# Differential attention: scores as two float32r products over stacked halves, blocks in order of heads

## The chip, the core and the metric

The kernel runs on one core of a Trainium2 chip. The metric is the device time of one execution in microseconds (us), the median of the runs; lower is better. A run's time is about 2 us more than the span that the profiler sees between the first and the last instruction.

## What is computed

A block of four mixers with a mixture of experts and two feed-forward parts, T = 512 tokens of width D = 1024, all in float32. The change touches the first mixer alone, differential attention with 8 heads; every head has two components of 64 dimensions for q and k, and a value of 128:

```python
q, k, v = jnp.split(x @ w_in, [2*H*dh, 4*H*dh], axis=-1)          # H = 8, dh = 64
q = rmsnorm(q.reshape(B, T, H, 2, dh), q_gain) * (dh ** -0.5)
k = rmsnorm(k.reshape(B, T, H, 2, dh), k_gain)
v = v.reshape(B, T, H, 2 * dh)
for s in range(0, T, QBLOCK):                                     # QBLOCK = 128
    e = s + QBLOCK
    sc = jnp.einsum('bqhcd,bkhcd->bhcqk', q[:, s:e], k[:, :e])
    dist = (jnp.arange(s, e)[:, None] - jnp.arange(e)[None, :])
    sc = jnp.where(dist >= 0, sc - slopes[:, None, None, None] * dist, -jnp.inf)
    p = jax.nn.softmax(sc, axis=-1)
    pd = p[:, :, 0] - lam * p[:, :, 1]
    outs.append(jnp.einsum('bhqk,bkhe->bqhe', pd, v[:, :e]))
o = rmsnorm(jnp.concatenate(outs, axis=1), subln) * (1.0 - lambda_init)
return o.reshape(B, T, H * 2 * dh) @ w_out
```

## The kernel before, in words

Differential attention is `stage_a` (line 397), the first of the program's stages; the experts follow, then the other mixers and feed-forward parts. TensorE's large products are split: weights and activations are each a high part (rounded to float32r) and a low remainder, and `mm3` (L131) issues three float32r products of 128 rows by 512 columns (in the profile L135 to L137 for products with weights stationary in one form, L139 to L141 in the other). The high part of a weight tile is an ACT copy (`wh`, L110), the low part a DVE subtraction (`wl`, L111). Weights come over the SP queue, 1 MB at a time, into three buffers `wr`.

`stage_a` works on two groups of four heads. `project(G)` (L437) makes q, k and v of a group: q and k are normalized per head component (`headnorm`, L443), transposed on TensorE (L464) and copied by one ACT instruction per block of 128 tokens (L465) into one tile `qt` or `kt` of four heads, each head with component 0 in rows 0 to 63 and component 1 in rows 64 to 127. `attend(G)` (L480) works in units of one block of 128 queries i and one head hh, blocks outermost:

```python
us = [(i, hh) for i in range(NT) for hh in range(4)]              # L552, before
```

A unit's `score` (L483) issues for each component c one float32 product over that component's 64 rows with n = 128(i+1) columns (L490). DVE adds the distance term and takes the minimum (`p<-s`, L491), scales it (L493); ACT takes the exponential (L494); DVE forms the reciprocal (L497, L498), scales (L499) and combines the two components (L500). `turn` (L502) transposes the result (L508) and copies it (L510) one unit later, `value` (L512) multiplies by v (L517) one more later. After the fourth head of a block, `onorm` (L523) normalizes 512 columns that hold one block of queries for four heads (L525 to L533), transposes them (L544) and makes their high and low parts `oh`, `ol` (L546, L547), which the output product `out(G)` needs in full, all four blocks of them, for each of its columns.

The lists of units are interleaved by `weave` (L177): `attend(0)` with all but eight units of `project(1)`; the first four units of `attend(1)` with these eight; the other twelve with `out(0)`, of which a part is kept for after the last unit. Then follow `out(1)` and the router. The order of each engine's instructions is then set by a scheduler in the framework, on which buffers and waits have their effect; so the change also moves instructions that it does not name. From the middle of `out(1)` to the end of the program the order of every engine is the same in both kernels (on PE the last 7316 rows).

`q_stack` (L662), `k_stack` (L672) and `halves` (L650) stand in the program already, for other mixers: `halves` makes the high part of a transposed tile by an ACT copy `nh` (L654) and the low part by a DVE subtraction `nl` (L655), with one buffer each; 64-row pieces of them are copied over the SP queue (128 KB each) into tiles of 128 rows: `qs` holds a component's high part above its low part, `kh` its high part twice, `kl` its low part twice (L667, L668, L682). Their scores are in `soft_heads` (L700): two float32r products of 128 rows, `kh` by `qs` and `kl` by `qs`, into one accumulator.

Of the kernel before, what the change touches and what calls it, by code (L numbers as in the profile page):

```python
# [4 lines left out]
F32 = mybir.dt.float32  # L5
# [3 lines left out]
AF = mybir.ActivationFunctionType  # L9
# [5 lines left out]
T, D, P = 512, 1024, 128  # L15
NT, NK = T // P, D // P
# [65 lines left out]
class K:  # L82
# [314 lines left out]
    def stage_a(self):  # L397
        nc, tc, a = self.nc, self.tc, self.a
        w_in, w_out = a["da_w_in"], a["da_w_out"]
        self.nmm, self.ns, self.ntp, self.npv = 4, 2, 1, 1  # L400
        with tc.tile_pool(name="pa", bufs=1) as pa:
            xv, wv = a["xT"].rearrange("(k p) t -> p k t", p=P), w_in.rearrange("(k p) n -> p k n", p=P)
# [8 lines left out]

            lv = pa.tile([P, 2, 64], F32, name="lv", tag="wk", bufs=7)
            ls = pa.tile([P, 2], F32, name="ls")
# [23 lines left out]
            def project(G, first=None):  # L437
                q = pa.tile([P, 4, T], F32, name="qt", tag="qt", bufs=2)
                k = pa.tile([P, 4, T], F32, name="kt", tag="kt", bufs=2)
                v = pa.tile([P, NT, 512], F32, name="v", tag="v", bufs=2)  # L440
                qkv[G] = (q, k, v)

                def headnorm(dst, gain, slopes=False):  # L443
                    def done(i, ps):
                        rt = self.rt[:, i:i + 1]
                        s = pa.tile([P, 512], F32, name="qs", tag="wk", bufs=7)
# [13 lines left out]

                        def turn():
                            tp = self.ptt()
                            for hh in range(4):
                                nc.tensor.transpose(tp[:, hh * P:(hh + 1) * P], s[:, hh * P:(hh + 1) * P], self.ident)  # L464
                            nc.scalar.activation(dst[:, :, i * P:(i + 1) * P], tp.rearrange("p (a b) -> p a b", a=4),  # L465
                                                 AF.Copy, scale=gain)
                        self.after(8, scale)
                        self.after(12, turn)
                    return done

                def vdone(i, ps):
                    nc.scalar.activation(v[:, i], ps, AF.Copy, scale=self.rt[:, i:i + 1])

                return (self.tm_cols(w_in, G * 512, 512, x, headnorm(q, gs[:, 0:1], True), first)
                        + self.tm_cols(w_in, 1024 + G * 512, 512, x, headnorm(k, self.vec("kg")))
                        + self.tm_cols(w_in, 2048 + G * 512, 512, x, vdone))

            def attend(G):
                q, k, v = qkv[G]
# [32 lines left out]
                def value(i, hh):  # L512
                    if hh == 0:
                        pvs[i] = self.pvt()
                    p = pt.pop((i, hh))
                    for j in range(i + 1):
                        nc.tensor.matmul(pvs[i][:, hh * P:(hh + 1) * P], lhsT=p[:, j * P:(j + 1) * P],  # L517
                                         rhs=v[:, j, hh * P:(hh + 1) * P], start=j == 0, stop=j == i,
                                         skip_group_check=True)
                    if hh == 3:  # L520
                        onorm(i, pvs.pop(i))

                def onorm(i, pv):  # L523
                    s = pa.tile([P, 512], F32, name="os", tag="wk", bufs=7)
                    nc.scalar.copy(s, pv)  # L525
# [11 lines left out]
                    def turn_o():  # L537
                        if G not in o:
                            o[G] = (self.x8("oh"), self.x8("ol"))
                        oh, ol = o[G]  # L540
                        qs = slice(i * P, i * P + P)
                        tp = self.ptt()
                        for hh in range(4):
                            nc.tensor.transpose(tp[:, hh * P:(hh + 1) * P], s[:, hh * P:(hh + 1) * P], self.ident)  # L544
                        tv = tp.rearrange("p (a b) -> p a b", a=4)
                        nc.scalar.activation(oh[:, :, qs], tv, AF.Copy, scale=gs[:, 1:2])  # L546
                        nc.vector.scalar_tensor_tensor(ol[:, :, qs], tv, gs[:, 1:2], oh[:, :, qs].bitcast(F32),  # L547
                                                       op0=OP.mult, op1=OP.subtract)
# [578 lines left out]
    def moe_begin(self, pool):  # L1127
# [12 lines left out]
        o = _CST["four"][0]  # L1140
        f = pool.tile([P, 388], F32, name="cr", tag="wk", bufs=7)
        nc.scalar.dma_start(f, a["cst"][:, o:o + 388])
# [7 lines left out]
    def zero_rows(self, pool):  # L1150

        z = pool.tile([P, T], F32, name="zr", tag="wk", bufs=7)
        self.nc.gpsimd.memset(z, 0.0)
# [4 lines left out]
    def route_step(self, pool):  # L1158
# [4 lines left out]
        def done(m, ps):  # L1163
# [5 lines left out]
            self.sumsq(m)  # L1169
            hg = pool.tile([P, T], F32, name="hg", tag="wk", bufs=7)  # L1170
            nc.scalar.activation(hg, self.h[:, m], AF.Copy, scale=g[:, m:m + 1])

            def turn():
# [9 lines left out]
                for i in range(NT):  # L1183
                    nc.tensor.transpose(tp[:, i * P:(i + 1) * P], hg[:, i * P:(i + 1) * P], self.ident)
                xk = pool.tile([P, T], F32, name="xk", tag="wk", bufs=7)
                nc.scalar.copy(xk, tp)
# [543 lines left out]
```

## Time and profile before

| what | value |
|---|---|
| median of 3 runs | 1909.3 us (1907.06 to 1910.37) |
| the profiled execution | 1910.65 us |
| its span, first to last instruction | 1908.9 us |
| mean granted TensorE clock | 0.988 |
| PE busy over the span | 1835.4 us, 96% |
| DVE, ACT, POOL busy | 69%, 51%, 12% |
| first score product of this attention | at 85.3 us |
| first of the second group of heads | at 181.5 us |
| last score's DVE step begins | at 231.95 us |
| last transposes of the normalized result | at 246.8 us |

PE is TensorE's matmul stream, PEld its weight loads, DVE VectorE, ACT ScalarE, POOL GpSimd, SP the engine whose queue issues most transfers. A busy time is the union of instructions' records; the matmul's recorded end lies after the point at which the next one can begin, so a price for a stretch of matmuls is the distance between starts. A float32 product leaves two records, a float32r product one. A wait has the form "who waits <- for whom".

### The profile page before, as it was taken

Reading aid. Unit: us, or ns where it says so; the run is one execution under the profiler, and the core shown is the slowest. Engines: PE = TensorE matmul, PEld = TensorE weight load, DVE = VectorE, ACT = ScalarE, POOL = GpSimd, SP = SyncE. Lnnn points to the kernel's source line nnn. Section 1 sums busy time; section 2 is a strip of 40 time slices with the busy share of each in tenths; the row PEclk is TensorE's granted clock in tenths of the full one; section 3 lists DMA queues with packets and bytes.
Section 4 is the critical chain, followed back from the end, with each engine's and each line's share of the span. In section 5 each row is a group of like instructions: output and inputs, shape, how many; then the busy total and the mean of one; then the engine's idle time right before and its main releaser. Section 6 shows DMA issues by size and latency. Waiting matters only on the chain.

```text
span 1908.9 us, 24634 instructions
## 1 busy us (share of the span) xinstructions
PE 1835.4 (96%) x8604; PEld 1448.6 (76%) x8605; DVE 1318.4 (69%) x2815; ACT 978.0 (51%) x1663; POOL 226.3 (12%) x277
## 2 busy tenths in 40 slices
PE   8999997999998999998999999999999999999997
PEld 6767685778887876675688888888777788888885
DVE  6586848999998689756677447744576667537753
ACT  5565656888885325346454224433376544324442
POOL 2000012222322302310200000012200100000001
PEclk9999998999999999999999999999999999999998
DMA  5511157999994454454232343234545233243331
GB/s 190 181 45 67 67 172 268 355 369 370 368 366 147 135 148 115 111 147 106 83 96 75 91 114 107 68 95 141 137 112 133 67 90 103 77 119 89 88 85 60
DMA packets 260098, 274.74 MB, mean 144 GB/s; under 512 B 14438, under 2 KB 175622, under 8 KB 259968
## 3 DMA queue, kind: packets, MB, share of 16 engines
q1 hardware_dynamic: 250688, 257.56, 44.1%
q0 software_dynamic: 5072, 10.00, 1.5%
q10 hardware_dynamic: 4208, 5.56, 0.8%
q8 instruction: 69, 1.13, 0.2%
q14 instruction: 61, 0.50, 0.1%
HBM read 238.19 MB, written 15.73 MB: 133 GB/s over the span
## 4 chain that ended last, share of the span: by engine, by line
PE 51%; DVE 2%; ACT 2%; DMA 1%; POOL 1%; SPq 1%; issue 1%; DVEq 0%; POOLq 0%; ACTq 0%
PE mm L137 14%; PE mm L135 14%; PE mm L136 14%; PE pv L727 2%; PE t L715 1%; PE s L700 1%; PE pv L1101 1%; PE mm L140 1%; PE mm L139 1%; PE mm L141 1%; DMA rsw<-qd 0%; SPq L391 0%; POOL rsw L392 0%; PE s L1067 0%; PE t L1086 0%
## 5 line engine op out<-in xcount | busy, mean ns | idle before, releaser
L110 ACT CAST wh<-wr 128x1024 fp32r<-128x1024 f32 (+5 forms) x335 | 306.6, 916 | 442.6 <-PE mm L136 318.8
L111 DVE TENSOR_TENSOR wl<-wr,wh 128x1024 fp32r<-128x1024 f32 (+4 forms) x332 | 356.8, 1078 | 196.4 <-ACT wh L110 193.7
L135 PE MATMUL mm<-xh,wh 128*128 128x512 f32 x952 | 372.9, 392 | 2.1 <-DVE h L384 1.8
L137 PE MATMUL mm<-xh,wl 128*128 128x512 f32 x952 | 372.9, 392 | 0.2 <-DVE wl L111 0.2
L136 PE MATMUL mm<-xl,wh 128*128 128x512 f32 x952 | 371.8, 391 | 0.0
L135 PEld LDWEIGHTS mm<-xh,wh 128*128 128x128 f32 x952 | 179.2, 188 | 40.0 <-issue 3.5
L137 PEld LDWEIGHTS mm<-xh,wl 128*128 128x128 f32 x952 | 179.1, 188 | 38.1 <-issue 1.1
L136 PEld LDWEIGHTS mm<-xl,wh 128*128 128x128 f32 x952 | 179.1, 188 | 36.1 <-issue 0.2
L111 DVE TENSOR_TENSOR wl<-wx,wh 128x1024 fp32r<-128x1024 f32 x123 | 151.3, 1247 | 11.7 <-ACT wh L110 5.6
L110 ACT CAST wh<-wx 128x1024 fp32r<-128x1024 f32 x134 | 139.5, 1050 | 27.6 <-PE mm L141 23.4
L139 PE MATMUL mm<-wh,xh 128*128 128x512 f32 (+2 forms) x352 | 132.0, 380 | 9.7 <-ACT wh L110 5.6
L135 PE MATMUL mm<-hh,wh 128*128 128x512 f32 x352 | 139.0, 395 | 0.0
L136 PE MATMUL mm<-hl,wh 128*128 128x512 f32 x352 | 138.9, 395 | 0.0
L137 PE MATMUL mm<-hh,wl 128*128 128x512 f32 x352 | 138.9, 395 | 0.0
L140 PE MATMUL mm<-wl,xh 128*128 128x512 f32 (+2 forms) x352 | 131.1, 373 | 4.3 <-DVE wl L111 4.2
L141 PE MATMUL mm<-wh,xl 128*128 128x512 f32 (+2 forms) x352 | 129.7, 369 | 0.0
L624 DVE TENSOR_TENSOR z<-mm,rb 128x512 f32<-128x512 f32 x88 | 60.4, 688 | 81.3 <-PE mm L137 81.3
L139 PE MATMUL mm<-wh,xeh 128*128 128x512 f32 x256 | 103.9, 406 | 0.8 <-ACT xeh L1361 0.8
L277 POOL TENSOR_TENSOR acc<-acc,sq 128x512 f32<-128x512 f32 x42 | 58.3, 1388 | 377.2 <-ACT sq L273 376.8
L141 PE MATMUL mm<-wh,xel 128*128 128x512 f32 x256 | 101.8, 398 | 0.0
L140 PE MATMUL mm<-wl,xeh 128*128 128x512 f32 x256 | 101.1, 395 | 0.0
L384 DVE TENSOR_TENSOR h<-mm,h 128x512 f32<-128x512 f32 x88 | 60.5, 690 | 50.4 <-PE mm L137 49.3
(406 smaller groups left out, 3352.3 us busy)
## 6 DMA issues: line engine op xcount, KB each, us to landing
wr<-in_ffn_w_up SPq DMA_DIRECT2D x88, 512.0 KB, 4.9
wx<-in_moe_w_gate SPq DMA_DIRECT2D x23, 1024.0 KB, 8.9
wx<-in_moe_w_up SPq DMA_DIRECT2D x22, 1024.0 KB, 9.7
wx<-in_moe_w_down SPq DMA_DIRECT2D x22, 1024.0 KB, 11.0
wr<-in_ffn_w_down SPq DMA_DIRECT2D x32, 704.0 KB, 4.6
wr<-in_da_w_in SPq DMA_DIRECT2D x11, 1024.0 KB, 5.1
wr<-in_even_w_in SPq DMA_DIRECT2D x11, 1024.0 KB, 5.5
wr<-in_moe_w_up SPq DMA_DIRECT2D x10, 1024.0 KB, 8.0
```

The costliest lines, as they stand in the source:

```text
L110: nc.scalar.copy(h, raw)
L111: (nc.gpsimd if eng else nc.vector).tensor_tensor(l, raw, h.bitcast(F32), op=OP.subtract)
L135: mm(out, lhsT=wh, rhs=xh, start=first, stop=False, skip_group_check=True)
L136: mm(out, lhsT=wh, rhs=xl, start=False, stop=False, skip_group_check=True)
L137: mm(out, lhsT=wl, rhs=xh, start=False, stop=last, skip_group_check=True)
L139: mm(out, lhsT=xh, rhs=wh, start=first, stop=False, skip_group_check=True)
L140: mm(out, lhsT=xh, rhs=wl, start=False, stop=False, skip_group_check=True)
L141: mm(out, lhsT=xl, rhs=wh, start=False, stop=last, skip_group_check=True)
L277: nc.gpsimd.tensor_tensor(self.acc, self.acc, sq, op=OP.add)
L384: self.nc.vector.tensor_tensor(self.h[:, m], ps, self.h[:, m], op=OP.add)
L624: nc.vector.tensor_tensor(z[:, 2:], ps, self.rb, op=OP.mult)
L727: nc.tensor.matmul(pv[64 * e:64 * e + 64, j * P:], lhsT=heads[u]["v"](j), rhs=pt[:, 4 * j:3 * j + 4], start=j == 0, stop=j == NT - 1, skip ...
```

## The change

The scores of differential attention take the form that `soft_heads` has. For every head, q and k are split into high and low halves and copied into stacks; a component's score block is two float32r products of 128 rows. The blocks go in order of heads, each head through its four query blocks; the normalized result is made per head. The tiles `qt` and `kt` hold two heads, three buffers each, so that the copy out of the transposes becomes two instructions. To make room, `p2` has two buffers for three, the work tiles `wk` six for seven, and the scratch for dynamic DMAs 2048 bytes for 8192. A head's stacks are asked for while the head ahead is at its blocks 1 (q) and 2 (k); those of each group's first head after its last k block.

```diff
+        self.nst, self.nsl = 4, 4
             def project(G, first=None):
-                q = pa.tile([P, 4, T], F32, name="qt", tag="qt", bufs=2)
-                k = pa.tile([P, 4, T], F32, name="kt", tag="kt", bufs=2)
+                q, k = [], []
...
-                            nc.scalar.activation(dst[:, :, i * P:(i + 1) * P], tp.rearrange("p (a b) -> p a b", a=4),
-                                                 AF.Copy, scale=gain)
+                            if i == 0:
+                                dst.extend(pa.tile([P, 2, T], F32, name=name, tag=name, bufs=3) for _ in range(2))
+                            for t, c in zip(dst, (0, 2 * P)):
+                                nc.scalar.activation(t[:, :, i * P:(i + 1) * P], tp[:, c:c + 2 * P].rearrange("p (a b) -> p a b", a=2),
+                                                     AF.Copy, scale=gain)
+                            if dst is k and i == NT - 1:
+                                self.after(2, lambda: prep(4 * G, 0))
+                                self.after(6, lambda: prep(4 * G, 1))
...
+            def prep(u, part):
+                t = qkv[u // 4][part][u % 4 // 2][:, u % 2]
+                if part == 0:
+                    stacks[u] = self.q_stack(pa, t)[0]
+                else:
+                    stacks[u] = [(q, *k) for q, k in zip(stacks[u], self.k_stack(pa, t))]
...
-                    p2 = p2s[i, hh] = pa.tile([P, 2, T], F32, name="p2", tag="p2", bufs=3)
+                    if hh < 3 and i in (1, 2):
+                        prep(4 * G + hh + 1, i - 1)
+                    p2 = p2s[i, hh] = pa.tile([P, 2, T], F32, name="p2", tag="p2", bufs=2)
                     for c in range(2):
-                        b = slice(64 * c, 64 * c + 64)
+                        q, *k = stacks[4 * G + hh][c]
                         s = self.pst()
-                        nc.tensor.matmul(s[:, :n], lhsT=q[b, hh, qs], rhs=k[b, hh, :n], start=True, stop=True)
+                        for m, t in enumerate(k):
+                            nc.tensor.matmul(s[:, :n], lhsT=q[:, qs], rhs=t[:, :n], start=m == 0, stop=m == 1)
...
-                    if hh == 3:
-                        onorm(i, pvs.pop(i))
+                    if i == NT - 1:
+                        onorm(hh, pvs.pop(hh))
...
-                us = [(i, hh) for i in range(NT) for hh in range(4)]
+                us = [(i, hh) for hh in range(4) for i in range(NT)]
...
-    nc = bacc.Bacc("TRN2", target_bir_lowering=False, num_devices=1, dynamic_dma_scratch_size=8192)
+    nc = bacc.Bacc("TRN2", target_bir_lowering=False, num_devices=1, dynamic_dma_scratch_size=2048)
```

How the order moves, at three places. In these rows the name left of the arrow is what is written, the names right of it what is read, with the tile's number; the line is that of the kernel concerned (in the changed kernel the score product is L510, the transposes of p2 L528, the value product L537, the transposes of the result L563, the stack copies L685, L686 and L700).

TensorE at the first scores, before: the two components of a unit (`s_841`, `s_846`) stand next to each other, between projection products.

```order
L139 MATMUL mm_678<-wh_768,xh1_108 128x512
L140 MATMUL mm_678<-wl_769,xh1_108 128x512
L141 MATMUL mm_678<-wh_768,xl1_110 128x512
L490 MATMUL s_841<-kt_122,qt_121 128x128
L490 MATMUL s_846<-kt_122,qt_121 128x128
L139 MATMUL mm_866<-wh_862,xh0_107 128x512
```

And in the change, at the same place (288 projection products stand ahead of the first score in both):

```order
L139 MATMUL mm_682<-wh_788,xh1_108 128x512
L140 MATMUL mm_682<-wl_789,xh1_108 128x512
L141 MATMUL mm_682<-wh_788,xl1_110 128x512
L510 MATMUL s_875<-kh_810,qs_776 128x128
L510 MATMUL s_875<-kl_813,qs_776 128x128
L139 MATMUL mm_902<-wh_898,xh0_107 128x512
L510 MATMUL s_881<-kh_816,qs_779 128x128
L140 MATMUL mm_902<-wl_899,xh0_107 128x512
L141 MATMUL mm_902<-wh_898,xl0_109 128x512
L139 MATMUL mm_902<-wh_898,xh0_107 128x512
```

Each component is now a couple of products on stacks that SP's copies must have filled, and projection products stand between them. The second group's first score, 534 projection and output products from the program's start before, has 559 ahead of it now.

TensorE at the end of the second group's attention, before, from one of the last units' transposes on (`t_2455`; its `mm` rows are output products of `out(0)`):

```order
L508 MATMUL t_2455<-ident_70,p2_2411 128x128 x4
L135 MATMUL mm_2507<-oh_1118,wh_2508 128x512
L136 MATMUL mm_2507<-ol_1119,wh_2508 128x512
L137 MATMUL mm_2507<-oh_1118,wl_2509 128x512
L517 MATMUL pv_2495<-v_838,pt_2433 128x128 x4
L517 MATMUL pv_2495<-v_838,pt_2460 128x128 x4
L508 MATMUL t_2488<-ident_70,p2_2438 128x128 x4
L135 MATMUL mm_2559<-oh_1118,wh_2560 128x512
L136 MATMUL mm_2559<-ol_1119,wh_2560 128x512
L137 MATMUL mm_2559<-oh_1118,wl_2561 128x512
L135 MATMUL mm_2559<-oh_1118,wh_2560 128x512
L517 MATMUL pv_2495<-v_838,pt_2493 128x128 x4
```

In the change, from the last score product on:

```order
L510 MATMUL s_2742<-kl_2547,qs_2488 128x512
L537 MATMUL pv_2662<-v_872,pt_2660 128x128
L137 MATMUL mm_2958<-oh_2444,wl_2960 128x512
L528 MATMUL t_2726<-ident_70,p2_2682 128x128 x2
L537 MATMUL pv_2818<-v_872,pt_2703 128x128
L537 MATMUL pv_2818<-v_872,pt_2729 128x128 x2
L528 MATMUL t_2753<-ident_70,p2_2707 128x128 x3
L537 MATMUL pv_2818<-v_872,pt_2757 128x128 x3
L563 MATMUL t_2786<-ident_70,os_2763 128x128 x4
...
L537 MATMUL pv_2818<-v_872,pt_2816 128x128 x4
L563 MATMUL t_2870<-ident_70,os_2829 128x128 x4
```

Between the last score and the last transposes of the result (`t_2870`) seven output products are left; before there were 47.

SP around the second group's first head, in the change (before, SP issues no copies between these loads):

```order
L128 DMA wr_1634<-in_da_w_in 128x4x512
L685 DMA qs_2016<-nh_2012 64x512
L686 DMA qs_2016<-nl_2013 64x512
L685 DMA qs_2019<-nh_2012 64x512
L686 DMA qs_2019<-nl_2013 64x512
L128 DMA wr_2327<-in_da_w_out 128x4x512
L128 DMA wr_2329<-in_da_w_out 128x4x512
L128 DMA wr_2931<-in_da_w_out 128x4x512
L700 DMA kh_2061<-nh_2057 64x512 x2
L700 DMA kl_2064<-nl_2058 64x512 x2
```

The copies of a head's k stack stand behind weight loads that were issued ahead of them on the same queue.

## Rows read from the trace of the kernel before

**Rows 1.** The page: span, busy times, and the clock by slices.
```profile
span 1908.9 us, 24634 instructions
PE 1835.4 (96%) x8604; PEld 1448.6 (76%) x8605; DVE 1318.4 (69%) x2815; ACT 978.0 (51%) x1663; POOL 226.3 (12%) x277
PEclk9999998999999999999999999999999999999998
```

**Rows 2.** Busy time by stretch: the attention's two halves.
```profile
core 0: us, PE busy (x) PEld busy (x) DVE busy (x) ACT busy (x) POOL busy (x), PEclk, DMA share, GB/s
85.00:181.00 96.00, 93.60 (x475) 66.41 (x474) 73.91 (x337) 57.98 (x127) 0.00 (x0) 1.00 0.17 55
181.00:254.00 73.00, 72.47 (x362) 49.95 (x361) 60.35 (x250) 43.32 (x111) 0.00 (x0) 1.00 0.25 83
```

**Rows 3.** The same view, the score products' line alone.
```profile
sum 169.00, PE 32.14 PEld 12.00; mean PE 16.07 PEld 6.00
```

**Rows 4.** Timeline of PE, two neighbouring components, a lone one, the last one.
```profile
130.47 1.13 PE L490 MATMUL s<-kt,qt 64*128 64x512 f32 x4
131.53 0.71 PE L517 MATMUL pv<-v,pt 128*128 128x128 f32 x4
...
226.41 1.12 PE L490 MATMUL s<-kt,qt 64*128 64x512 f32 x2
227.47 0.66 PE L544 MATMUL t<-ident,os 128*128 128x128 f32 x4
228.05 0.69 PE L490 MATMUL s<-kt,qt 64*128 64x512 f32 x1
```

**Rows 5.** Timeline of PE in a later mixer with stacked scores.
```profile
749.57 0.39 PE L700 MATMUL s<-kh,qs 128*128 128x512 f32 x1
749.80 0.39 PE L700 MATMUL s<-kl,qs 128*128 128x512 f32 x1
750.03 0.40 PE L137 MATMUL mm<-xh,wl 128*128 128x512 f32 x1
```

**Rows 6.** Busy time of that line over eight such heads.
```profile
725.00:832.00 107.00, 16.00 (x64) 10.14 (x64) 1.00 0.47 122
```

**Rows 7.** The halves in that mixer: tile nh, durations in ns and waits.
```profile
L654 ACT CAST nh<-qa x4: 603/606/622, 843.6 to 887.3; 128x512 fp32r<-128x512 f32 x4
L655 DVE TENSOR_TENSOR nl<-ka,nh x4: 685/688/689, 849.7 to 892.7; 128x512 fp32r<-128x512 f32 x4
DMA to landing us min/median/max: 2.2/2.4/5.2
```

**Rows 8.** The score tile there: what ended idle time before it (us, times).
```profile
  DMA kl<-nl: 2.4, 2
  DMA kh<-nh: 2.4, 2
```

**Rows 9.** DMA issues: KB each, median us to landing.
```profile
wr<-in_da_w_in SPq DMA_DIRECT2D x11, 1024.0 KB, 5.1
qs<-nh SPq DMA_DIRECT2D x32, 128.0 KB, 2.2
qs<-nl SPq DMA_DIRECT2D x32, 128.0 KB, 2.6
```

**Rows 10.** Timeline of PE behind the last score: output products, last transposes.
```profile
243.14 0.39 PE L137 MATMUL mm<-oh,wl 128*128 128x512 f32 x1
243.36 0.39 PE L135 MATMUL mm<-oh,wh 128*128 128x512 f32 x1
...
246.31 0.39 PE L136 MATMUL mm<-ol,wh 128*128 128x512 f32 x1
246.82 0.63 PE L544 MATMUL t<-ident,os 128*128 128x128 f32 x4
```

**Rows 11.** Timeline of DVE: the last score's step and its result's normalization.
```profile
231.95 0.68 DVE L491 CUSTOM_DVE_ANT_0 p<-s,c_dist 128x512 f32<-128x512 f32 x1
232.56 0.09 DVE L491 DVE_READ_ACCUMULATOR2_ANT st<- 128x1 f32 x1
...
235.68 0.74 DVE L500 SCALAR_TENSOR_TENSOR p<-p,rc 128x512 f32<-128x512 f32 x1
...
240.46 0.69 DVE L529 TENSOR_REDUCE oss<-sq 128x4 f32<-128x512 f32 x1 [1.38 <-ACT sq L527]
...
245.98 0.69 DVE L533 TENSOR_TENSOR os<-os,rsq 128x512 f32<-128x512 f32 x1
```

**Rows 12.** Waits between 84 and 242 us (us, times, longest).
```profile
ACT p L494 <- DVE st L493: 21.7, 27, 4.4
DVE p L491 <- PE s L490: 13.6, 12, 5.4
```

More of the change, by code (lines that the diff above doesn't have):

```diff
@@ L410, in stage_a @@
             nc.sync.dma_start(dist, a["cst"][:, _CST["dist"][0]:_CST["dist"][0] + T])
-            lv = pa.tile([P, 2, 64], F32, name="lv", tag="wk", bufs=7)
+            lv = pa.tile([P, 2, 64], F32, name="lv", tag="wk", bufs=6)
             ls = pa.tile([P, 2], F32, name="ls")
@@ L472, in vdone @@
                     nc.scalar.activation(v[:, i], ps, AF.Copy, scale=self.rt[:, i:i + 1])
-                return (self.tm_cols(w_in, G * 512, 512, x, headnorm(q, gs[:, 0:1], True), first)
-                        + self.tm_cols(w_in, 1024 + G * 512, 512, x, headnorm(k, self.vec("kg")))
+                return (self.tm_cols(w_in, G * 512, 512, x, headnorm(q, "qt", gs[:, 0:1], True), first)
+                        + self.tm_cols(w_in, 1024 + G * 512, 512, x, headnorm(k, "kt", self.vec("kg")))
                         + self.tm_cols(w_in, 2048 + G * 512, 512, x, vdone))
+            stacks = {}
+            def prep(u, part):
[4 more added lines that the diff above has]
+                    stacks[u] = [(q, *k) for q, k in zip(stacks[u], self.k_stack(pa, t))]
             def attend(G):
-                q, k, v = qkv[G]
+                v = qkv[G][2]
                 pvs, pt, p2s = {}, {}, {}
@@ L512, in value, with onorm @@
                 def value(i, hh):
-                    if hh == 0:
-                        pvs[i] = self.pvt()
+                    if i == 0:
+                        pvs[hh] = self.pvt()
                     p = pt.pop((i, hh))
                     for j in range(i + 1):
-                        nc.tensor.matmul(pvs[i][:, hh * P:(hh + 1) * P], lhsT=p[:, j * P:(j + 1) * P],
+                        nc.tensor.matmul(pvs[hh][:, i * P:(i + 1) * P], lhsT=p[:, j * P:(j + 1) * P],
                                          rhs=v[:, j, hh * P:(hh + 1) * P], start=j == 0, stop=j == i,
                                          skip_group_check=True)
-                    if hh == 3:
-                        onorm(i, pvs.pop(i))
-                def onorm(i, pv):
-                    s = pa.tile([P, 512], F32, name="os", tag="wk", bufs=7)
+                    if i == NT - 1:
+                        onorm(hh, pvs.pop(hh))
+                def onorm(hh, pv):
+                    s = pa.tile([P, 512], F32, name="os", tag="wk", bufs=6)
                     nc.scalar.copy(s, pv)
@@ L540, in turn_o @@
                         oh, ol = o[G]
-                        qs = slice(i * P, i * P + P)
                         tp = self.ptt()
[L543 to L547, printed above, removed]
+                        for i in range(4):
+                            nc.tensor.transpose(tp[:, i * P:(i + 1) * P], s[:, i * P:(i + 1) * P], self.ident)
+                        nc.scalar.activation(oh[:, hh], tp, AF.Copy, scale=gs[:, 1:2])
+                        nc.vector.scalar_tensor_tensor(ol[:, hh], tp, gs[:, 1:2], oh[:, hh].bitcast(F32),
                                                        op0=OP.mult, op1=OP.subtract)
@@ L1140, in moe_begin @@
         o = _CST["four"][0]
-        f = pool.tile([P, 388], F32, name="cr", tag="wk", bufs=7)
+        f = pool.tile([P, 388], F32, name="cr", tag="wk", bufs=6)
         nc.scalar.dma_start(f, a["cst"][:, o:o + 388])
@@ L1150, in zero_rows @@
     def zero_rows(self, pool):
-        z = pool.tile([P, T], F32, name="zr", tag="wk", bufs=7)
+        z = pool.tile([P, T], F32, name="zr", tag="wk", bufs=6)
         self.nc.gpsimd.memset(z, 0.0)
@@ L1169, in done @@
             self.sumsq(m)
-            hg = pool.tile([P, T], F32, name="hg", tag="wk", bufs=7)
+            hg = pool.tile([P, T], F32, name="hg", tag="wk", bufs=6)
             nc.scalar.activation(hg, self.h[:, m], AF.Copy, scale=g[:, m:m + 1])
@@ L1184, in turn @@
                     nc.tensor.transpose(tp[:, i * P:(i + 1) * P], hg[:, i * P:(i + 1) * P], self.ident)
-                xk = pool.tile([P, T], F32, name="xk", tag="wk", bufs=7)
+                xk = pool.tile([P, T], F32, name="xk", tag="wk", bufs=6)
                 nc.scalar.copy(xk, tp)
```

4 lines of the change are left out of this document (2 added, 2 removed).

## The prediction

> **What bounds the kernel now.** First the page: PE is busy for 1835.4 of 1908.9 us and its clock stands at its upper level in nearly every slice, while no other engine passes 76% [rows 1]. Time is therefore gained by giving PE less to do, or lost by making it wait. Then the stretches: the change acts between the first score at 85 us and the point, near 254 us, where the attention's last result has gone through PE. There PE is busy for 93.60 of 96.0 us in the first half (four heads) and for 72.47 of 73.0 in the second; DVE stands at 73.91 (77%) and 60.35 (83%) [rows 2]. So PE sets the pace, DVE is next, and in the second half it is near. The clock is 1.00 in both, so no price here mixes levels. Behind this point the order of every engine is the same in both kernels, up to the prefetch of two weight tiles; what is won or lost by 254 us should reach the end as it is, and the sum is made for these 169.0 us alone.
>
> **Scores.** Their line is busy for 32.14 us in the two halves [rows 3]. That is not yet what they cost. In the timeline a unit's two components of 512 columns, four records, start at 130.47 and the next instruction at 131.53, so 1.06 us for both; a lone component, two records, costs 1.06 too (226.41 to 227.47) [rows 4]. Two products over 64 rows each, one in the lower and one in the upper half, thus run side by side when they are neighbours. The record, at 1.13, is longer than the distance by 6%; by the same share the 32.14 are about 30.1 us of PE's time.
>
> The new form is in the trace already, in another mixer: `kh` starts at 749.57, `kl` at 749.80, and the next product at 750.03, so a couple of 512 columns costs 0.46 us and its last record runs 0.16 over into what follows [rows 5]. Eight heads with one component each make 32 couples of all four sizes and are busy for 16.00 us [rows 6]; less 32 times 0.16 for the overrun that is 10.9, and with two components per head 21.8. If every size went by columns at the rate of 512 (0.46 times 10/4 a component, sixteen of them) it would be 18.4. I take 21.1, nearer to the sum over whole heads: the scores lose **9.0 us** (bounds 8.3 and 11.7), half in each half.
>
> [...]
>
> **Making the stacks.** Sixteen ACT casts of 0.61 us and sixteen DVE subtractions of 0.69 [rows 7], 9.8 and 11.0 us in all; DVE's next instruction starts about 0.61 after one of that length (231.95 to 232.56 [rows 11]). Ten subtractions fall into the first half, six into the second. In the first half DVE then has 73.91 + 10 x 0.61 = 80.0 us in some 98: covered. ACT goes from 101.3 of 169 us to some 113 with the halves and eight more copies out of the transposes; covered. The 96 copies of 128 KB over SP land in 2.2 to 2.6 us [rows 7, 9]; with a DMA share of 0.17 and 0.25 [rows 2] the bytes have room. Three costs remain on the path.
>
> *First stacks.* Head 0's copies follow its last k block at once; PE waits for cast, subtraction and landing, about 0.61 + 0.61 + 2.4 and the issue of the later of eight copies, less the projection products that the scheduler put between. In the other mixer the scores waited twice for `kh` and twice for `kl`, 2.4 us in all for each [rows 8]. I take **+1.5** (0 to 4).
>
> *The seam.* `nh` and `nl` have one buffer. At the second group's start three casts (k of head 4, q of head 5, k of head 5) follow each other on ACT with only a few exponentials and copies between; a cast must wait until the copies out of the last one have landed, up to 5.2 us [rows 7], and the exponentials behind it on ACT wait too. Projection and output products stand ready on PE. I take **+1.0** (0 to 4).
>
> *Head order.* Before, the last score's DVE step starts at 231.95, its combined result is done some 4.5 us later, its normalization runs from the reduction at 240.46 to the scaling at 245.98 [rows 11], and the last transposes start at 246.82; below this chain of 14.9 us PE worked through output products every 0.2275 us, with a gap of only some 0.3 us ahead of the transposes [rows 10]. In the new order 7 of the 47 output products behind the last score are left there. The same chain takes perhaps 11.5 us with DVE emptier, at most 14.9 as in the row; PE's work in it is 7 products at 0.2275, 11 value products and 13 transposes at about 0.11 each, 4.3 us. So PE idles for 7.2 to 10.6 us; some of it falls into gaps that it had. I take **+7.0** (5 to 10.6).
>
> **What costs nothing.** The split copy of `qt` and `kt` sits on ACT, which had 43.32 of 73.0 us to do in the fuller half. Six `wk` and two `p2` buffers: a third of `p2` let a score's DVE step run ahead of the transposes; with two, a score waits for the transposes of the one before last. DVE's waits for PE were 13.6 us in all, and ACT's for DVE 21.7 [rows 12]; I put nothing on it apart from what the slower rival holds. The smaller scratch concerns the experts' gathers and scatters on POOL, busy 12% [rows 1]; nothing is counted, and what speaks against it would show at 290 to 580 us, not here.
>
> **The sum.** First half: 96.0, plus 25 products that now stand ahead of the second group's first score (559 against 534, 5.7 us), less 4.5, plus 1.5: 98.7. Second half: 73.0 - 5.7 - 4.5 + 7.0 = 69.8; the seam 1.0. Together 169.5 against 169.0, so **+0.5 us**. DVE in the second half has 60.35 + 6 x 0.61 = 64.0 us in 69.8, 92%: it fits, but barely, and this is the weakest step. The profiled execution is 1910.65 us (1908.9 of span and 1.75 around it); it stands 1.35 above the median of 1909.3, to which I add the difference: 1909.8. Over the bounds, scores at their best with the least of each cost give 1909.3 - 11.7 + 5 = 1902.6; at the worst of each 1909.3 - 8.3 + 4 + 4 + 10.6 = 1919.6.
>
> **Rivals.**
>
> *DVE takes over (slower).* In the second half PE's work is now 62.8 us without the tail, DVE's 64.0. DVE never reached more than 83% of a half; its order is fixed, each unit goes from PE to DVE to ACT and back, and only two `p2` buffers decouple it. The point from which this decides is 64.0/69.8, 92%: if DVE can keep only 83% as in the row, the half takes 64.0/0.83 = 77.1 in place of 69.8, and the time is 1909.8 + 7.3 = 1917. For it: the last score's DVE step at 231.95 [rows 11] came some 3 us after its product at 228.05 [rows 4], so DVE was already behind there. Against it: the 83% were set by PE, not by DVE. Chance 0.22.
>
> *The scores give more, or the tail less (faster).* [...] Chance 0.30, of it 0.08 by the rule.
>
> *Stacks behind weights (slower).* [...] Chance 0.10. [...]
>
> *No effect of the edit itself* is excluded by the order: couples on stacks stand where the old products stood.
>
> **How the numbers follow.** The forecast, 1905 to 1914, has 0.38; faster 0.30, DVE 0.22, late stacks 0.10. A measurement of this kernel tells about 0.2%, 3.8 us, from no change: faster means under 1905.5, slower over 1913.1. Of the forecast's 0.38 some 0.02 falls on each side beyond; the faster cases reach up to 1905.5 and hold 0.29 beyond it; the slower ones hold 0.30. That gives 0.31 faster, 0.36 same, 0.33 slower. The range leaves out the extremes of both sides: 1901 to 1918.
>
> **What would show it.** In the changed profile: the score line busy for about 30 us in the two halves by its records, though 21 by distances between starts (a couple of 512 columns at 0.46); the second group's first score near 184 us; PE idle for 6 to 9 us between the last score and the last transposes of the result; these waits named for ACT or DVE, not DMA. Waits of the score products for `kh`, `kl` or `qs` of more than 4 us in all would show late stacks; DVE at over 90% and PE waiting for its steps in the second half, the DVE rival. The forecast is wrong if the result leaves 1901 to 1918, and its reasons are wrong if a difference arises after 290 us, where the order is the same.

## The result, and the profile after

The changed kernel takes 1922.73 us in the median (1921.63 to 1923.2, 4 runs) against 1909.61 before: slower by 13.1 us, ratio 1.007 with a 95% interval of 1.0053 to 1.0088. That is above the range of 1901 to 1918; the forecast was 0.5 us more.

The page and the stretches of the changed kernel, to be held against [rows 1 to 3]; the last line is the score line alone (columns as there):

```profile
span 1921.4 us, 24892 instructions
PE 1832.6 (95%) x8604; PEld 1463.1 (76%) x8605; DVE 1328.7 (69%) x2831; ACT 986.9 (51%) x1695; POOL 224.2 (12%) x277
...
85.00:181.00 96.00, 93.52 (x492) 76.24 (x493) 79.84 (x349) 62.51 (x143) 0.00 (x0) 0.98 0.45 126
181.00:254.00 73.00, 63.15 (x328) 49.73 (x327) 59.60 (x237) 42.42 (x110) 0.00 (x0) 0.93 0.59 166
...
sum 169.00, PE 31.84 PEld 22.53; mean PE 15.92 PEld 11.27
```

PE is busy for 2.8 us less over the span, part of that at a lower clock, and the span is 12.5 us longer. In the first half PE is as busy as before, with a clock of 0.98 for 1.00. In the second, PE's 72.47 busy us of 73.0 have become 63.15, and the granted clock, 1.00 before, is 0.93.

The new scores at a granted clock of 1.00 (223 to 225 us), from the timeline of PE (start, duration, instruction, idle before):

```profile
223.85 0.40 PE L510 MATMUL s<-kh,qs 128*128 128x512 f32 x1
224.08 0.40 PE L510 MATMUL s<-kl,qs 128*128 128x512 f32 x1
224.32 0.39 PE L537 MATMUL pv<-v,pt 128*128 128x128 f32 x2
```

A couple of 512 columns costs 0.47 us (0.46 in the other mixer [rows 5]). PE waits for the first head's stacks twice, in component 0's `kl` and in component 1's `kh`, 2.53 us together:

```profile
83.16 0.22 PE L510 MATMUL s<-kh,qs 128*128 128x128 f32 x1
85.02 0.33 PE L510 MATMUL s<-kl,qs 128*128 128x128 f32 x1 [1.64 <-DMA kl<-nl]
85.18 0.44 PE L139 MATMUL mm<-wh,xh 128*128 128x512 f32 x1
86.52 0.30 PE L510 MATMUL s<-kh,qs 128*128 128x128 f32 x1 [0.89 <-DMA kh<-nh]
```

Behind these waits the granted clock falls for a while, to 0.70 and 0.50 in the stretches from 86 to 88 and from 88 to 90 us:

```profile
86.00:88.00 2.00, 1.48 (x5) 1.22 (x6) 0.20 (x1) 1.46 (x4) 0.00 (x0) 0.70 0.30 68
88.00:90.00 2.00, 2.00 (x8) 1.71 (x7) 0.96 (x4) 0.49 (x1) 0.00 (x0) 0.50 0.60 137
```

Most of the loss is in the second group of heads. The end of it on PE, from the last score product on:

```profile
241.50 0.40 PE L510 MATMUL s<-kl,qs 128*128 128x512 f32 x1
...
245.11 0.52 PE L528 MATMUL t<-ident,p 128*128 128x128 f32 x3 [1.30 <-DVE st L513]
246.29 0.94 PE L537 MATMUL pv<-v,pt 128*128 128x128 f32 x6 [0.66 <-ACT pt L530]
249.85 1.09 PE L563 MATMUL t<-ident,os 128*128 128x128 f32 x4 [2.62 <-DVE os L553]
251.71 1.22 PE L135 MATMUL mm<-oh,wh 128*128 128x512 f32 x2 [0.78 <-ACT oh L564]
252.73 1.06 PE L528 MATMUL t<-ident,p 128*128 128x128 f32 x4
...
255.29 1.91 PE L537 MATMUL pv<-v,pt 128*128 128x128 f32 x8
262.45 1.08 PE L563 MATMUL t<-ident,os 128*128 128x128 f32 x4 [5.25 <-DVE os L553]
```

And on DVE, to be held against [rows 11]:

```profile
243.75 0.68 DVE L511 CUSTOM_DVE_ANT_0 p<-s,c_dist 128x512 f32<-128x512 f32 x1
...
246.78 0.75 DVE L520 SCALAR_TENSOR_TENSOR p<-p,rc 128x512 f32<-128x512 f32 x1
...
249.01 0.69 DVE L553 TENSOR_TENSOR os<-os,rsq 128x512 f32<-128x512 f32 x1
...
258.52 0.69 DVE L549 TENSOR_REDUCE oss<-sq 128x4 f32<-128x512 f32 x1 [6.08 <-ACT sq L547]
```

The last unit's combined probabilities are ready at 247.5, yet PE transposes them (L528) at 252.73. In PE's order the transposes of the third head's normalized result (L563, 249.85) stand ahead of them, and wait 2.62 us for DVE's scaling at 249.01; then the second output product's first steps wait for that head's high part. Only then comes the last unit, with its value products, copy, normalization and a wait of 5.25 us. From the last score's step on DVE to the last transposes it is 18.7 us, against 14.9 before. The waits between 181 and 266 us say the same (us, times, longest):

```profile
PE t L563 <- DVE os L553: 9.0, 4, 5.2
...
PE mm L135 <- ACT oh L564: 2.3, 3, 0.8
```

Where PE loses time shows in two stretches of each kernel, from the second group's first score product to the last one and from there to the last transposes of the result; first before, then the change:

```profile
181.50:228.60 47.10, 46.69 (x223) 29.14 (x222) 40.12 (x190) 30.70 (x87) 0.00 (x0) 1.00 0.26 90
228.60:246.80 18.20, 18.10 (x105) 14.63 (x104) 15.71 (x52) 9.55 (x20) 0.00 (x0) 1.00 0.00 1
...
183.60:241.50 57.90, 54.14 (x285) 43.03 (x284) 49.46 (x200) 36.23 (x96) 0.00 (x0) 0.97 0.70 200
241.50:262.40 20.90, 10.12 (x44) 7.78 (x42) 11.30 (x44) 6.55 (x16) 0.00 (x0) 0.72 0.00 0
```

Before, PE idles for 0.4 and 0.1 us in them; now for 3.8 and 10.8, and the clock in the end is 0.72.

No wait for stack copies stands among the large ones. The experts' first gather is issued at 305.1 in place of 292.8, 12.3 us late, and the span ends 12.5 late: all the loss was made ahead of that point.

### The profile page after: what moved, and what is told of

Its sections match the earlier page's. It is cut to its first block, busy times and chain, and to the rows that moved or that the text cites. A ratio compares the mean times of both kernels' runs of the same rounds, so it can differ in the third digit from the quotient of the medians.

```text
span 1921.4 us, 24892 instructions
## 1 busy us (share of the span) xinstructions
PE 1832.6 (95%) x8604; PEld 1463.1 (76%) x8605; DVE 1328.7 (69%) x2831; ACT 986.9 (51%) x1695; POOL 224.2 (12%) x277
## 4 chain that ended last, share of the span: by engine, by line
PE 54%; DVE 6%; DMA 2%; ACT 2%; POOL 2%; issue 1%; SPq 1%; DVEq 0%; POOLq 0%; ACTq 0%
PE mm L135 15%; PE mm L137 15%; PE mm L136 15%; PE pv L745 3%; PE t L733 1%; DVE wl L111 1%; PE mm L140 1%; PE mm L139 1%; PE mm L141 1%; DVE sc L908 1%; PE s L718 1%; DVE m L907 1%; PE pv L1119 1%; POOL rsw L392 1%; SPq L391 1%
## 5 line engine op out<-in xcount | busy, mean ns | idle before, releaser
L277 POOL TENSOR_TENSOR acc<-acc,sq 128x512 f32<-128x512 f32 x42 | 58.3, 1388 | 392.8 <-ACT sq L273 392.4
```

Of the source, the lines that this page charges most:

```text
L277: nc.gpsimd.tensor_tensor(self.acc, self.acc, sq, op=OP.add)
```

## Experiments

Ratios are to the kernel before, measured beside each run, with their 95% interval; 0.001 is 1.9 us. The changed kernel is 1.007.

**Undoing the parts.** The order of heads alone, with old scores and buffers:

```diff
-                us = [(i, hh) for i in range(NT) for hh in range(4)]
+                us = [(i, hh) for hh in range(4) for i in range(NT)]
...
-                    if hh == 3:
-                        onorm(i, pvs.pop(i))
+                    if i == NT - 1:
+                        onorm(hh, pvs.pop(hh))
```

> The kernel before with the order of heads alone (units by head, normalization per head), old float32 scores, old buffers. Theory 'order': the output products are used up ahead of the end of the attention and the last chain stands bare, so this alone costs 10 us or more against the kernel before (1920 or above), since the scores save nothing here. Theory 'DVE': the loss comes from the sixteen added subtractions on DVE, so this is within 4 us of the kernel before (1906 to 1914).

1925.04 us, 1.0084 (1.0067 to 1.0101): 16 us. The order carries the whole loss; the rest of the change, taken together, does not add to it. The trace of this run shows where:

```profile
240.00:250.00 10.00, 10.00 (x51) 7.12 (x51) 7.73 (x28) 5.52 (x15) 0.00 (x0) 1.00 0.38 112
250.00:260.00 10.00, 4.83 (x27) 3.21 (x25) 4.16 (x16) 2.49 (x4) 0.00 (x0) 1.00 0.52 199
260.00:270.00 10.00, 6.91 (x22) 5.56 (x23) 5.23 (x14) 4.20 (x7) 0.85 (x1) 0.50 0.00 0
270.00:280.00 10.00, 10.00 (x40) 8.33 (x39) 1.29 (x2) 3.02 (x6) 1.57 (x2) 0.64 0.43 133
```

The kernel before has PE busy for 39.88 of these 40 us and the clock at 1.00. Here PE idles for 8.3 us, and the 16.9 us in which it is busy behind 260 run at 0.50 and 0.64, which by these rows costs an estimated 7 us more. By this estimate about half of the order's loss is idling and about half is clock.

The buffers alone (`p2` 3 to 2, `wk` 7 to 6, scratch 8192 to 2048):

> The kernel before with the change's buffers alone (two p2 for three, six wk for seven, scratch of 2048 bytes). If buffers are a cause: 4 us or more above the kernel before (1913 or above), with DVE waiting for transposes. Theories 'order' and 'DVE' both expect within 2 us (1908 to 1912).

1911.06 us, 1.0007 (0.9997 to 1.0017). With the old scores they cost nothing that can be told from noise.

The stacks without their subtractions (this run leaves out the low halves of q and k):

```diff
...
+            nc.scalar.copy(h, t)
+            return h.bitcast(F32), h.bitcast(F32)
...
```

> The changed kernel without the sixteen DVE subtractions for the stacks: the low rows of the stacks are filled from the high half (leaves out the low halves of q and k), same copies, same products. Theory 'DVE' (second half paced by DVE at 83% of its time): six subtractions of 0.61 us at that share give back 4.4 us in the second half, and 2 to 4 in the first, so 1915 to 1918. Theory 'order': the bare end stays as it is; 1920 to 1923.

1924.79 us, 1.0084 (1.0067 to 1.01). Taking 11 us of work off DVE gives nothing. The DVE rival, whose sum had come close, is out as the cause of this loss.

The order in the first group alone, then the new scores and the order in the first group alone (`heads = G == 0` chooses between the two forms of the unit list, the value products and the normalization):

> The kernel before with the order of heads in the first group of four heads alone. Theory 'bare end' (what costs is the end of the second group, where output products were cover): within 2 us of the kernel before (1906 to 1911), as projection products lie beside the first group's end. Rival 'order everywhere' (each head's short units run PE dry in both groups): about half of the 16 us of the order alone, 1914 to 1918.

> The changed kernel with the new scores and the order of heads in the first group alone; the second group has float32 scores and blocks in order, with the change's buffers. Theory 'bare end': the loss goes away and the first half's gain of 2.8 us stays, 1905 to 1909. Rival 'order everywhere' or a cost of the stacks: 1913 or above.

1910.45 us, 1.0011 (1.0002 to 1.0021), and 1908.39 us, 0.9997 (0.9987 to 1.0007). By difference some 14 of the order's 16 us belong to the second group. Against the kernel before, the second run gained no more than can be told from nothing; against the first run, which has the same order, it stands 2.7 us lower, and the intervals overlap.

**Shortening the bare end.** The last head's blocks from the largest to the smallest:

```diff
...
-                us = [(i, hh) for hh in range(4) for i in range(NT)]
+                us = [(i, hh) for hh in range(4) for i in (range(NT) if hh < 3 or G == 0 else reversed(range(NT)))]
```

> The changed kernel with the last head's four blocks taken from the largest to the smallest, so that the last unit has 128 columns in place of 512. Theory 'order': the bare chain behind the last score gets shorter by the difference of the steps between the sizes (DVE minimum 0.4, exponential 0.3, scaling 0.2, combining 0.5, copy 0.3, transposes and values 0.7 at half clock: 2 to 3 us), so 1919 to 1921. Theory 'DVE': DVE's sum of work is the same, so within 1 us of the changed kernel (1922 to 1924).

1920.21 us, 1.0061 (1.0044 to 1.0077), 1.7 us less than the changed kernel by the ratios, and the intervals overlap: the sign expected, no proof.

More of the second output product beside the end, by splitting its weights two column tiles at a time, and both edits together:

```diff
...
+                if wide and q % 2 == 0:
+                    hl[0] = self.split(raw[0][:, :, q * P:(q + 2) * P], [P, 4, 2 * P])
...
```

> The changed kernel with the weights of the output products split into high and low parts two column tiles at a time, so that four column tiles of the second output product can be under way on the first heads' results while the last head is finished: 36 output products of that kind ahead of the last transposes of the result in place of 18. Theory 'bare end': 18 products of 0.2275 us and more full clock, 4 to 8 us less than the changed kernel (1915 to 1919). Rival (the chain alone sets the end, and PE's order keeps the products from running in its gaps): within 2 us of 1922.7.

> Both at once: weights split two column tiles at a time, and the last head's blocks from the largest to the smallest. Theory 'bare end': the two gains add, 6 to 11 us less than the changed kernel (1912 to 1917), still above the kernel before. Rival: no more than the 2.5 us that the descending order gave by itself (1920).

1927.75 us, 1.0109 (1.0083 to 1.0135), and 1922.6 us, 1.007 (1.0053 to 1.0088). Not what was expected: 18 more products did run ahead of the last transposes, and these came at 263.82, no earlier. What they could have saved was lost behind them, as this stretch of the wide split shows (columns as in [rows 2]):

```profile
270.00:280.00 10.00, 10.00 (x38) 8.93 (x38) 2.52 (x3) 2.81 (x5) 2.56 (x2) 0.50 0.09 26
```

PE is busy for the whole of it at a granted clock of 0.50, behind 40 us, from 225 to 265, of which it had been busy for 25.9.

**Holding cover back.** Half of the first group's output products wait for a unit near the end (here the second unit of the last head):

```diff
+                    if G and (i, hh) == (1, 3):
+                        nc.vector.tensor_scalar(gate, st[:, 0:1], 0.0, 1.0, op0=OP.mult, op1=OP.add)
...
-        nc.scalar.copy(h, raw)
+        if gate is not None:
+            nc.scalar.activation(h, raw, AF.Copy, scale=gate)
+        else:
+            nc.scalar.copy(h, raw)
...
```

> The changed kernel with half of the first group's output products (48, 10.9 us of PE) held back: the copies that make the high parts of their weights read a scale of 1.0 that DVE writes behind the last unit's score. Theory 'cover spent early' (PE's order runs these products ahead of the attention's last units, so that the last score comes late and the chain behind it is bare): the last score moves ahead by up to 10 us and the products lie beside the chain; 8 us or more are won, 1909 to 1915, unless the wait for the last score leaves a hole of its own ahead of them. Rival 'the chain of units sets the end whatever PE runs beside it': the last score does not move, 1920 to 1925.

> The same, with the products held back to the second unit of the last head. Theory 'cover spent early': 1907 to 1914, at or under the run held to the last score, since the hole ahead of the release is shorter. Rival: 1920 to 1925.

> The same, held back to the last unit of the last head but one. Theory 'cover spent early': part of the products is spent ahead of the last score again, 1910 to 1918. Rival: 1920 to 1925.

> Held back to the second unit of the last head, and that head's blocks from the largest to the smallest. Theory 'cover spent early': the gain of the descending order, 2.5 us where the end was bare, shrinks to 0 to 2 us where the products cover the chain; 1905 to 1914. Rival: 1918 to 1921, the descending order's own gain.

1923.69, 1922.75, 1924.01 and 1922.79 us: 1.0076 (1.0059 to 1.0093), 1.0079 (1.0062 to 1.0096), 1.0086 (1.0068 to 1.0104) and 1.0075 (1.0058 to 1.0092). All four miss; my theory that cover was spent too early falls. In the second of them 66 output products stand between the last score and the last transposes, where the changed kernel has seven, and no time is won. With the products out of the way the units did not come sooner. Held to the last score, the stretch in which they stood nearly alone:

```profile
217.00:248.00 31.00, 19.65 (x89) 16.26 (x88) 20.75 (x96) 14.42 (x42) 0.00 (x0) 0.70 0.41 115
```

PE, DVE and ACT are all partly idle, so it is waiting, not work, that fills the time; and the largest of PE's waits there are those of the end again, now at two heads:

```profile
PE t L570 <- DVE os L560: 4.7, 2, 3.1
...
PE t L535 <- DVE ol L572: 2.7, 2, 1.6
```

(L570 and L572 are the result's transposes and low part there, L560 its scaling, L535 the units' transposes.) The result's transposes wait for DVE, and the next unit's wait until DVE has read them out of the one PSUM buffer for transposes.

**Moving the result's transposes.** The third theory. In the unit list a unit's value products come four units behind its score (`ATT = (1, 4)`), and `onorm` asks for the transposes of its result once 4 us of unit cost have been emitted (the woven output units count too). In the new order every head's result is made in the unit that also scores the next head's fourth block and turns its third: 0.45 x (4 x 1.0 + 3 x 0.35 + 4 x 1.0) = 4.07, by the program's cost formula. That is over 4, so the result's transposes are emitted in that very unit, ahead of the next unit's. In blocks, at the same place of the last block, the unit costs 0.45 x (4 x 1.0 + 4 x 0.35 + 3 x 1.0) = 3.78, and they come one unit later.

```diff
-                    self.after(4, turn_o)
+                    self.after(7, turn_o)
```

> The changed kernel with a head's transposes of the normalized result asked for later (7 in place of 4 in the units' own cost), in both normalizations of the attention: on PE they then stand behind the last units' transposes, not ahead of them. Theory 'results ahead of units' (PE works in order and has one PSUM buffer for transposes, so a head's result, whose normalization takes some 7 us on DVE and ACT, holds up the next head's small units and at the end the last unit, which waited 5 us there): 4 to 9 us less than the changed kernel, 1914 to 1919. Rival (each unit's own steps through DVE and ACT set the pace): within 2 us, 1921 to 1925.

1911.3 us, 1.0006 (0.9995 to 1.0018): one number takes off 12 us by the ratios, more than I expected. PE's end now has the last unit's transposes ahead of the third head's result:

```profile
242.93 0.60 PE L528 MATMUL t<-ident,p 128*128 128x128 f32 x4
...
244.58 0.60 PE L563 MATMUL t<-ident,os 128*128 128x128 f32 x4
...
251.12 0.63 PE L563 MATMUL t<-ident,os 128*128 128x128 f32 x4 [1.56 <-DVE os L553]
```

PE's waits for the result, 9.0 us above:

```profile
PE t L563 <- DVE os L553: 1.6, 1, 1.6
```

The number moves two things at once: the results stand behind the units, and more output products are left behind the last score, 32 in place of seven.

With the cover held back as well, and, on the changed kernel, with two PSUM buffers for transposes and one for scores (`self.nmm, self.ns, self.ntp, self.npv = 4, 1, 2, 1`):

> The later transposes, and the first group's last 48 output products held back to the second unit of the last head. Theory 'results ahead of units': with the units no longer held up the last score can come earlier, and the products lie beside the chain; 1908 to 1916, less than the later transposes alone. Rival: 1920 to 1925, as when they were held back by themselves.

> The changed kernel with two PSUM buffers for transposes and one for scores, in place of one and two. If the single buffer for transposes is what holds up the units: 4 us or more less, 1914 to 1919, though the scores' single buffer takes some of it back. If PE's order holds them up whatever buffers there are, or the scores' second buffer is worth more: 1922 or above.

1913.52 us, 1.0023 (1.0013 to 1.0034): holding back does not help here either; it stands above the later transposes alone, with overlapping intervals. What this run does show is the units' own pace. With the same products held back, the second group's score steps on DVE take 60.9 us from the first to the last with early transposes of the result and 52.3 with later ones. 1918.99 us, 1.005 (1.0033 to 1.0067): 3.8 us less by the ratios, at the edge of what was expected and with overlapping intervals, so a share of the buffer stays unproven beside PE's order.

The controls: the same number in the order alone, a larger one in the changed kernel, and the same in the kernel before.

> The kernel before with the order of heads alone and the later transposes of the result (7 for 4). Theory 'results ahead of units': the 16 us of the order alone go by 8 to 14 us, to 1911 to 1917; with the old scores it stays 2 us or so above the changed kernel with later transposes (1911.3). Rival (the later transposes help only beside the stacks): 1921 or above.

> The changed kernel with the transposes of the result asked for at 10 in place of 4: 51 products of the output are left behind the last score's, against 32 at 7. Theory 'results ahead of units': as good as 7 or up to 4 us better, 1907 to 1912; a wait of the second output product for late results would show as more, to 1915. Rival 'bare end only': 1917 or above.

> The kernel before, blocks in order, with the later transposes (7 for 4). There a result does not stand ahead of short units at the end of the attention, so theory 'results ahead of units' expects no change, within 2 us (1907.5 to 1911.5). If it gains 4 us or more, the later transposes are a gain by themselves and not a cure of what the order of heads brought.

1909.8 us, 0.9999 (0.9989 to 1.001): the 16 us of the order alone are gone, so the cure does not need the stacks, and it is fuller than expected. 1905.35 us, 0.9985 (0.9974 to 0.9997): the changed kernel with 10 is the first version below the kernel before, by about 2.9 us (0.6 to 5). 1911.44 us, 1.0009 (0.9999 to 1.002): before the change the same edit gains nothing. So the later transposes cure what the order of heads brought and are no gain by themselves. In the version with 10 the second half is PE's again, though not as full as before:

```profile
181.00:254.00 73.00, 67.64 (x368) 53.98 (x366) 63.30 (x247) 46.33 (x117) 0.38 (x1) 0.98 0.57 166
```

## Why the prediction was wrong

*What bounds the kernel*: right. The second half was where PE had room to lose, and nothing arose behind 300 us.

*Scores, 9.0 us less*: the price of a couple was right (0.47 against 0.46). The line's busy time cannot show the saving (31.84 against 32.14), since its records, 0.40 us long, overlap what starts 0.24 later. Summed over the traces as distances between starts, the scores cost 29.6 us before and an estimated 22.2 after, reckoned at a granted clock of 1.00, 7.5 less. No run shows the rule to which the prediction gives 0.08 of the chance for faster; what the runs showed is 0.94 us for two couples of 512 columns where the two old products took 1.06. Little of this saving became time. With the same later delay of 7 the changed kernel (1.0006) stands above the order alone (0.9999), with overlapping intervals, and with 10 (0.9985) it stands 2.7 us below. What took the saving is waiting: with the delay of 7, from the first score to the experts' first gather, PE idles 18.2 us in the changed kernel and 9.8 in the order alone, and its time at a granted clock of 0.50 costs an estimated 5.3 and 0.8.

*First stacks, +1.5*: too low. PE waited 1.64 and 0.89 us, and the low clock behind these waits, by the rows from 86 to 90 us, cost an estimated 1.5 us more. The first copies took up to 6.4 us to land, where 2.2 to 2.6 had been taken. The second group's first score came 2.1 us later (183.6 against 181.5), but the attention's first score had come 2.1 us earlier (83.2 against 85.3): the first half grew by 4.3 us, where 2.7 had been forecast. *The seam, +1.0*: one cast waited 1.0 us for copies, on ACT; PE has no wait for stacks between 181 and 266 us. *Buffers, split copies and scratch at nothing*: the buffers and the scratch are right within the interval. The copies out of the transposes held PE once, for 1.04 us at 71.9, where it did not wait before.

*Head order, +7.0*: this is the step that failed. I priced the bare end by its idling alone, and put the clock at nothing ("The clock is 1.00 in both, so no price here mixes levels."). The idling was near the forecast of 7.2 to 10.6 us: 8.3 in the run with the order alone, and 10.6 between the last score's step and the last transposes in the changed kernel. What the sum did not hold is the low clock behind the gaps, 0.50 and 0.64 in the order alone, an estimated 7 us there. Nor did it hold the third head's normalization: I took the chain's length from the kernel before, 11.5 to 14.9 us, and it took 18.7, since that head's result stands in PE's order ahead of the last unit. The rows of order showed it: in the excerpt of the change's end the result's transposes `t_2786` stand ahead of the value products on `pt_2816`, the last unit's. I counted the products between the rows and did not ask what each row waits for.

The whole can be added up from the trace, from the attention's first score to the experts' first gather. PE idles for 26.3 us in place of 9.7. Its busy time at a granted clock of 0.50, 21.7 us in place of 1.55, costs an estimated 10.9 us in place of 0.8, half of it being counted as lost (the output products at the end stand 0.43 us apart for 0.23). What is left, PE's work reckoned at a granted clock of 1.00, is 12.2 us less; 7.5 of it are the scores', where the rest comes from is not shown. Together that is 14.5 us more, less the 2.1 by which the first score came earlier: 12.3, the delay of the gather. (The same products stand ahead of the first score in all runs, and in their traces it comes at 82.1 to 87.0 us, so these 2.1 are not the change's.)

From the first score's step of the second group to the last it is 58.3 us against 49.5. This is not in itself a slowing of the units: 118 projection and output products stand in that stretch, where there were 81, and the 37 more make 8.4 us at 0.2275; PE idles 4.0 us in it, against 0.4. In the order alone it idles 0.8 there. With the later transposes of the result it still idles 4.3, while the end's 10.6 fall to 2.5.

*The named rivals*: DVE taking over gave 1917; it and late stacks both have the right sign. DVE is excluded as the cause of this loss by the run without subtractions; late stacks are excluded by the waits, apart from the 2.5 us at the first head. The sixteen copies into `kh` and `kl` that SP issued from 179.7 to 196.7 us, behind three weight loads, landed in 2.3 to 2.4 us; no trace shows that a load ahead of them on the queue was what made the first head's copies slower.

What stays open: how the 12 us that the later transposes give back divide between a result that no longer holds up the units and the products left behind the last score, 32 for seven (58 for 30 in the order alone). Products there are not enough by themselves: with 66 held back and early transposes nothing was won. The share of the one buffer for transposes is open too.

## What to carry to other kernels

In PE's order here, a row that waited for a chain on other engines held up what stood behind it: the last unit, ready at 247.5, was transposed at 252.7. When a change reorders work, read for every moved group not only what covers it but what now stands behind its wait. A delay in units of emitted cost (4 against 3.78 or 4.07) belongs to the order that it was set for, and must be tuned anew with it. Price a gap by its length and by the clock behind it (here 0.50). Cover alone did not cure a chain that was held up: with products held back for the end, PE idled 11.4 of 31 us among the units.

## What the runs showed of the hardware

The granted clock fell behind the gaps. At the end of the changed kernel's attention it was 0.50 from 260.9 to 267.7 us, though PE's transposes had begun at 262.45, and the output products there stand 0.43 us apart in place of 0.23:

```profile
264.31 1.22 PE L135 MATMUL mm<-oh,wh 128*128 128x512 f32 x2 [0.78 <-ACT oh L564]
265.33 0.63 PE L136 MATMUL mm<-ol,wh 128*128 128x512 f32 x1
265.76 0.63 PE L137 MATMUL mm<-oh,wl 128*128 128x512 f32 x1
```

and in the wide split ten fully busy microseconds ran at 0.50; with the order alone PE was busy from 270 to 280 us at a mean of 0.64, behind 20 us of which it had idled 8.3. So more than the gaps was lost with these stretches of idling: part of what followed ran at a granted clock of 0.50.

Two neighbouring float32 products of 64 rows, one on rows 0 to 63 and one on rows 64 to 127, take no longer than a lone one (1.06 us at 512 columns [rows 4]). Two couples of float32r products over 128 rows, for the same two components, take 0.94 (223.85 to 224.32, 0.47 each). That leaves little to gain where components are neighbours. Ten of the 64 components stood alone before, each at a pair's full price, and they are part of the 7.5 us saved.
